# Full-height second score products and deinterleaved up weights in a hybrid decoder block with 32 experts

## Chip, core and metric

One core of one Trainium2 chip. The metric is the device time of one execution in microseconds; the median of several executions is given, and one further execution was profiled. Everything is computed in fp32 by splitting operands into a high and a low part (type fp32r) and adding three, or where one operand is packed two, products.

## The reference, cut to what matters

One layer on x of shape (1, 1024, 1024): a combined input projection feeds a stick-breaking attention (8 heads of 64) and an HGRN2 recurrence (4 heads of 128); both are projected, merged by sigmoid gates, projected again and normalised. Then a router picks 4 of 32 experts for each token, and each expert is a clamped SwiGLU. The two places that the change touches:

```python
def stick_breaking_attention(q, k, v):
    for blk in range(T // SB_BLOCK):                      # blocks of 128 queries
        t0, t1 = blk * SB_BLOCK, (blk + 1) * SB_BLOCK
        z = jnp.einsum('bhtd,bhsd->bhts', qf[:, :, t0:t1], kf[:, :, :t1]) * scale
        mask = jnp.arange(t1)[None, :] < (t0 + jnp.arange(SB_BLOCK))[:, None]
        log_keep = jnp.where(mask, jax.nn.log_sigmoid(-z), 0.0)
        log_after = lax.cumsum(log_keep, axis=3, reverse=True) - log_keep
        weights = jnp.where(mask, jnp.exp(jax.nn.log_sigmoid(z) + log_after), 0.0)
        outs.append(jnp.einsum('bhts,bhsd->bhtd', weights, vf[:, :, :t1]))

def expert_block(args):
    xblk, e = args
    hcat = xblk @ w_up[e] + b_up[e]                       # 1024 -> 2048
    x_glu = jnp.minimum(hcat[:, 0::2], SWIGLU_LIMIT)      # even columns
    x_lin = jnp.clip(hcat[:, 1::2], -SWIGLU_LIMIT, SWIGLU_LIMIT)
    act = x_glu * jax.nn.sigmoid(SWIGLU_ALPHA * x_glu) * (x_lin + 1.0)
    return act @ w_down[e] + b_down[e]
```

## The kernel before

The stages follow each other: projections of x and the HGRN chunks (to about 555 us of the span), the attention (to about 786 us), branch projections and merge, output projection and router (to about 1060 us), the experts (to about 2530 us), the last normalisation. `split` (L122) casts to the high part on ACT (L125) and subtracts it from the source on DVE or POOL (L126) to get the low part. `mm3` (L128) is the projections' triple of products (L130, L131, L132).

**Attention** (`sb_attention`, L551). Queries go in blocks of 128, i = 0 to 7; block i has 128 (i + 1) keys. A unit is a group of heads of one block (HEADS: 8, 4, 2, 2, 1, 1, 1, 1 heads), 43 units in all. The q tile of a block, 128 rows by 8 heads by 128 queries, holds a head's 64 channels twice: the high part on the rows of the head's own half (even heads 0 to 63, odd heads 64 to 127), the low part on the other half. `load_q` (L569) brings the raw queries, two transfers, `split_q` casts them (ACT, L576) and subtracts (DVE, L579). The keys' high part `kh` has them on both halves, the low part `kl` has the two heads of a pair on the two halves of one tile. So a score tile z takes two products: L611 on all 128 rows (high and low q with high k), and L612 on the 64 rows of the head's half (high q with low k). ACT turns z into `keep` and `take` by two sigmoids (L615, L616), POOL masks the diagonal (L620), DVE scans `keep` and multiplies it into `take` (L629, L631), PE transposes (L642), ACT or DVE copies (L645, L647), PE multiplies with v (L664, 64 columns wide).

```python
for s in range(n + 3):
    scores(s); stick(s - 1); turn(s - 2); average(s - 3)     # with yields between
```

`lockstep` (L70) mixes this stream with a second one, `beside` (L1688): the gate projections that are left (pj, L130 to L132) and then the turning of the branches (L730). It fixes the order of PE's instructions by estimated costs.

**Experts** (`experts`, `expert`). The experts are sorted by load; places 0 to 17 have capacities of 204 down to 134 tokens ("wide"), places 18 to 31 have 128. SEQ alternates wide and others. Weights come in raw pieces of 1 MB (six buffers, all on SP's queue, L1198); `part` splits a piece of 128 x 1024 into wh and wl (8 buffers each) six pieces ahead of its use, every fifth piece's subtraction on POOL, the others on DVE. In a wide expert the weight is the stationary operand. Its up product takes even columns (g = 0) and odd ones (g = 1) apart, each with 128 columns of the piece, every second word:

```python
for g in range(2):
    nc.tensor.matmul(ps[g][:, :2 * n], wh[:, kk, g::2], x[:, k]...)       # L1220
    nc.tensor.matmul(ps[g][:, :n], wl[:, kk, g::2], x[:, k, 0], ...)      # L1222
```

The down product (`down_parted`, L1269 and L1271) has the same shapes with 128 words in a row. There are 18 x 16 = 288 wide up pieces with 8 such pairs each, 2304 pairs. The 14 other experts use the weight as the moving operand (L1303 to L1305).

Of the kernel before, what the change touches and what calls it, by code (L numbers as in the profile page):

```python
# [9 lines left out]
F32 = mybir.dt.float32  # L10
F32R = mybir.dt.float32r
# [10 lines left out]
KT = D // 128  # L22
# [38 lines left out]
SBH = 8  # L61
# [53 lines left out]
class Block:  # L115
# [382 lines left out]
    def sb_tiles(self):  # L498
# [3 lines left out]
        self.kl = sp.tile([128, 4, T], F32R, name="kl")  # L502
        self.sv = sp.tile([128, NB, 512], F32, name="sv")

    def sb_jobs(self):

        nc = self.nc
        self.q_d = self.dram("q_scratch", (512, T))

        def ev_k(c):  # L510
            def go(ps, ct, half):
                p = 2 * c + ct
                t = slice(512 * half, 512 * half + 512)
                for i in range(2):
                    r, o = slice(64 * i, 64 * i + 64), slice(64 - 64 * i, 128 - 64 * i)
                    self.split(self.kh[r, 2 * p + i, t], self.kl[r, p, t], ps[r])
                    (nc.vector.tensor_copy if i else nc.scalar.copy)(self.kh[o, 2 * p + i, t], ps[r])
            return go

        def ev_q(c):  # L520
            def go(ps, ct, half):
                s = self.work.tile([128, 512], F32, name="pe", bufs=2)
                nc.scalar.copy(s, ps)
                r = 256 * c + 128 * ct
                nc.gpsimd.dma_start(self.q_d[r:r + 128, 512 * half:512 * half + 512], s)
            return go

        def ev_v(c):
            def go(ps, tb):
                nc.vector.tensor_copy(self.sv[:, tb, 256 * c:256 * c + 256], ps)  # L530
            return go

        jobs = []
        for c in range(2):
            jobs.append((OFF_SQ + 256 * c, (0, 1), ev_q(c)))
            jobs.append((OFF_SK + 256 * c, (0, 1), ev_k(c)))
        jobs += [(OFF_SV + 256 * c, None, ev_v(c)) for c in range(2)]
        return jobs
# [18 lines left out]
    def sb_attention(self):  # L557

        nc, wk = self.nc, self.work
# [3 lines left out]
        after = dict(zip(BLOCKS, BLOCKS[1:]))  # L563
        st = {}

        def load_q(i):
            raw = wk.tile([128, SBH, 128], F32, name="qraw", bufs=2)
            for r in (slice(0, 64), slice(64, 128)):
                nc.sync.dma_start(raw[r], self.q_d[:, 128 * i:128 * i + 128].rearrange("(h p) t -> p h t", p=64))  # L569
            st["raw", i] = raw  # L570

        def split_q(i):

            q = wk.tile([128, SBH, 128], F32R, name="q", bufs=2)
            raw = st.pop(("raw", i))
            nc.scalar.copy(q, raw)  # L576
            for k in range(2):
                s = (slice(64 - 64 * k, 128 - 64 * k), slice(k, None, 2))
                nc.vector.tensor_tensor(q[s], raw[s], q[s].bitcast(F32), op=OP.subtract)  # L579
            st["q", i] = q  # L580

        def heads(u):

            i, h0 = units[u]
            h = range(h0, h0 + HEADS[i])
            return [*h[::2], *h[1::2]]

        def scores(u):
            i, h0 = units[u]
            m, S = HEADS[i], 128 * (i + 1)  # L590
            if u == 0:
                load_q(i)
                split_q(i)
            if i in after and h0 == 0:
                load_q(after[i])
            if i in after and h0 + m >= 6 and h0 < 6:
                split_q(after[i])
            q = st["q", i]
            take = wk.tile([128, T], F32, name="take", bufs=4)
            keep = wk.tile([128, T], F32, name="keep", bufs=3)  # L600
            per = max(1, min(m // 2, 512 // S))
            hs = heads(u)
            for g in range(0, m, per):
                for s0 in range(0, S, 512):
                    n = min(512, S - s0)
                    ps = self.sps.tile([128, 512], F32, name="z", bufs=2)
                    for k in range(per):
                        h = hs[g + k]
                        r = slice(64 * (h % 2), 64 * (h % 2) + 64)
                        o, s = ps[:, S * k:S * k + n], slice(s0, s0 + n)  # L610
                        nc.tensor.matmul(o, q[:, h], self.kh[:, h, s], start=True, stop=False)  # L611
                        nc.tensor.matmul(o, q[r, h], self.kl[r, h // 2, s], start=False, stop=True)  # L612
                    w = n + S * (per - 1)
                    d = slice(S * g + s0, S * g + s0 + w)
                    nc.scalar.activation(keep[:, d], ps[:, :w], AF.Sigmoid, scale=-0.125)  # L615
                    nc.scalar.activation(take[:, d], ps[:, :w], AF.Sigmoid, scale=0.125)  # L616

            for t, fill in ((keep, 1.0), (take, 0.0)):
                t = t[:, :m * S].rearrange("p (h s) -> p h s", h=m)[:, :, S - 128:]
                nc.gpsimd.affine_select(t, t, pattern=[[0, m], [-1, 128]], compare_op=OP.is_gt, fill=fill,  # L620
                                        base=0, channel_multiplier=1)
            st[u] = [keep, take]
# [58 lines left out]
        n = len(units)  # L681
# [473 lines left out]
    def expert(self, n, e, rows, bias, choice):  # L1155
        nc, wk, a = self.nc, self.work, self.a
        blocks = [(s, min(128, n - s)) for s in range(0, n, 128)]
        nb = len(blocks)
        wide, parted = n > 128, n >= PARTED
        f = "A" if wide else "B"  # L1160
        X = {}
# [39 lines left out]
        def part(kind, c, q, width, kn):  # L1201

            per = 2048 // width // kn
            r = X["raw", kind, c, q // per][:, kn * (q % per):kn * (q % per) + kn]
            wh = wk.tile([128, kn, width], F32R, name="wh", bufs=8)
            wl = wk.tile([128, kn, width], F32R, name="wl", bufs=8)
            self.pieces += 1
            self.split(wh, wl, r, nc.gpsimd if self.pieces % POOLED == 0 else nc.vector)
            X[kind, c, q] = wh, wl

        def up_wide(c, q):
            wh, wl = X.pop(("up", c, q))
            x = X["x"]
            if q == 0:
                X["ps"] = [self.eps.tile([128, 512], F32, name="mm", bufs=6) for g in range(2)]
            ps = X["ps"]
            for kk in range(4):
                k = 4 * q + kk
                for g in range(2):
                    nc.tensor.matmul(ps[g][:, :2 * n], wh[:, kk, g::2], x[:, k].rearrange("p a n -> p (a n)"),  # L1220
                                     start=k == 0, stop=False)
                    nc.tensor.matmul(ps[g][:, :n], wl[:, kk, g::2], x[:, k, 0], start=False, stop=k == KT - 1)  # L1222
            if q == 0:
                return
            if c == 0:
                X["a"] = wk.tile([128, KT, 2, n], F32R if parted else F32, name="aTA", bufs=1)
            gl = wk.tile([128, 2, 256], F32, name="gl", bufs=3)[:, :, :n]
            for g in range(2):
                nc.scalar.activation(gl[:, g], ps[g][:, n:2 * n], AF.Identity, bias=bias(g, c))  # L1229
                nc.vector.tensor_add(gl[:, g], gl[:, g], ps[g][:, :n])  # L1230
            nc.vector.tensor_scalar(gl[:, 0], gl[:, 0], SWIGLU_LIMIT, None, op0=OP.min)
            nc.vector.tensor_scalar(gl[:, 1], gl[:, 1], SWIGLU_LIMIT + 1.0, 1.0 - SWIGLU_LIMIT,
                                    op0=OP.min, op1=OP.max)
            X["gl", c] = gl
# [125 lines left out]
        def piece(product, kind, c, q, width, kn, parted=True, after=()):  # L1360
            per = 2048 // width // kn
            return ((fetch, kind, c, q // per, width) if q % per == 0 else None,
                    (part, kind, c, q, width, kn) if parted else None, (product, c, q), list(after))

        if wide:
            up = [piece(up_wide, "up", c, q, 256, 4, True,
                        [(1, gate_wide, c)] + [(2, part_wide, c)] * parted if q else [])
                  for c in range(8) for q in range(2)]
# [4 lines left out]
        else:  # L1373
            up = [piece(up_narrow, "up", c, q, 512, 2, True, [(1, gate_narrow, c), (3, turn_act, c)] if q == 3 else [])
                  for c in range(4) for q in range(4)]
# [382 lines left out]
```

## Time and profile before

| | |
|---|---|
| median of 3 runs | 2603.86 us (2602.51 to 2604.72) |
| the profiled execution's own time | 2603.79 us |
| its span | 2602.2 us |
| busy: PE, PE weight loads, DVE, ACT, POOL | 2464.0, 2180.7, 1870.6, 1454.7, 869.2 us |
| mean granted TensorE clock | 0.974 |

PE is TensorE's matmuls and PEld its weight loads, which overlap them; DVE, ACT, POOL and SP are the vector, scalar, GpSimd and sync engines. Matmuls are pipelined and their ends are modelled, so the time that one costs is read from its start to the next one's start. A view by windows gives busy time of each engine in a stretch, the mean granted clock as a share of full speed, the share of the 16 DMA engines' time and GB/s.

### The profile page before, as it was taken

Reading aid. Unit: us, or ns where it says so; the run is one execution under the profiler, and the core shown is the slowest. Engines: PE = TensorE matmul, PEld = TensorE weight load, DVE = VectorE, ACT = ScalarE, POOL = GpSimd, SP = SyncE. Lnnn points to the kernel's source line nnn. Section 1 sums busy time; section 2 is a strip of 40 time slices with the busy share of each in tenths; the row PEclk is TensorE's granted clock in tenths of the full one; section 3 lists DMA queues with packets and bytes.
Section 4 is the critical chain, followed back from the end, with each engine's and each line's share of the span. In section 5 each row is a group of like instructions: output and inputs, shape, how many; then the busy total and the mean of one; then the engine's idle time right before and its main releaser. Section 6 shows DMA issues by size and latency. Waiting matters only on the chain. (4 is left out here: it accounts for less than half of the span.)

```text
span 2602.2 us, 41853 instructions
## 1 busy us (share of the span) xinstructions
PE 2464.0 (95%) x15476; PEld 2180.7 (84%) x15476; DVE 1870.6 (72%) x3107; ACT 1454.7 (56%) x2513; POOL 869.2 (33%) x744
## 2 busy tenths in 40 slices
PE   8999999999989987799999999999999999999992
PEld 8898888886767765789989999999998999889981
DVE  3217673347775477687888789888888888888885
ACT  3213332325564311576777677776677777777772
POOL 1011110003221324344434344444444444444443
PEclk9999999999999998899999999999999999999996
DMA  5321233233123523898998989999899998999973
GB/s 165 96 81 53 79 109 101 65 77 96 51 86 114 175 89 112 261 304 285 302 310 292 286 272 305 314 302 290 272 305 299 312 299 287 302 308 321 320 226 138
DMA packets 426788, 550.57 MB, mean 212 GB/s; under 512 B 21382, under 2 KB 312342, under 8 KB 426580
## 3 DMA queue, kind: packets, MB, share of 16 engines
q1 hardware_dynamic: 403684, 476.76, 56.3%
q0 software_dynamic: 22608, 70.05, 9.4%
q8 instruction: 123, 2.02, 0.3%
q10 hardware_dynamic: 288, 1.05, 0.2%
q14 instruction: 85, 0.70, 0.1%
HBM read 496.33 MB, written 51.47 MB: 211 GB/s over the span
## 5 line engine op out<-in xcount | busy, mean ns | idle before, releaser
L126 DVE TENSOR_TENSOR wl<-raw,wh 128x1024 fp32r<-128x1024 f32 x671 | 882.8, 1329 | 201.9 <-ACT wh L125 197.8
L125 ACT CAST wh<-raw 128x1024 fp32r<-128x1024 f32 x824 | 845.0, 1046 | 70.7 <-PE pj L269 20.6
L1220 PE MATMUL mm<-xTA,wh 128*128 128x292 f32 (+16 forms) x2304 | 616.8, 355 | 0.0
L126 POOL TENSOR_TENSOR wl<-raw,wh 128x1024 fp32r<-128x1024 f32 x153 | 379.6, 2481 | 508.8 <-ACT wh L125 467.2
L1222 PE MATMUL mm<-xTA,wl 128*128 128x146 f32 (+16 forms) x2304 | 544.6, 236 | 0.0
L1222 PEld LDWEIGHTS mm<-xTA,wl 128*128 128x128 f32 x2304 | 454.9, 197 | 0.5
L1220 PEld LDWEIGHTS mm<-xTA,wh 128*128 128x128 f32 x2304 | 450.4, 196 | 0.8
L1269 PE MATMUL mm<-aTA,wh 128*128 128x292 f32 (+16 forms) x1152 | 299.4, 346 | 3.2 <-POOL aTA L126 3.2
L1271 PE MATMUL mm<-aTA,wl 128*128 128x146 f32 (+16 forms) x1152 | 270.9, 235 | 0.0
L1271 PEld LDWEIGHTS mm<-aTA,wl 128*128 128x128 f32 x1152 | 220.1, 191 | 0.6
L1269 PEld LDWEIGHTS mm<-aTA,wh 128*128 128x128 f32 x1152 | 216.6, 188 | 4.4 <-POOL aTA L126 3.9
L130 PE MATMUL pj<-xh,wh 128*128 128x512 f32 x512 | 209.5, 409 | 0.0
L126 POOL TENSOR_TENSOR aTA<-gl,aTA 128x146 fp32r<-128x146 f32 (+16 forms) x144 | 112.5, 789 | 285.0 <-ACT aTA L125 276.5
L132 PE MATMUL pj<-xh,wl 128*128 128x512 f32 x512 | 201.3, 393 | 0.0
L131 PE MATMUL pj<-xl,wh 128*128 128x512 f32 x512 | 200.7, 392 | 0.0
L1303 PE MATMUL mm<-wh,xTB 128*128 128x512 f32 x448 | 187.8, 419 | 0.0
L1305 PE MATMUL mm<-wh,xTB 128*128 128x512 f32 x448 | 176.3, 393 | 0.0
L1304 PE MATMUL mm<-wl,xTB 128*128 128x512 f32 x448 | 175.0, 391 | 0.0
L1229 ACT ACTIVATE gl<-mm,bup 128x146 f32<-128x146 f32 (+16 forms) x288 | 96.9, 388 | 116.9 <-PE mm L1222 115.0
L1239 DVE TENSOR_TENSOR gl<-gl 128x146 f32<-128x146 f32 (+16 forms) x144 | 113.6, 789 | 10.9 <-ACT gl L1238 10.7
L132 PEld LDWEIGHTS pj<-xh,wl 128*128 128x128 f32 x512 | 96.7, 189 | 21.4
L130 PEld LDWEIGHTS pj<-xh,wh 128*128 128x128 f32 x512 | 96.8, 189 | 20.7 <-issue 2.5
(350 smaller groups left out, 4664.5 us busy)
## 6 DMA issues: line engine op xcount, KB each, us to landing
raw<-in_expert_w_up_dram SPq DMA_DIRECT2D x252, 1024.0 KB
raw<-in_expert_w_down_dram SPq DMA_DIRECT2D x128, 1024.0 KB
raw<-in_w_in_dram SPq DMA_DIRECT2D x56, 512.0 KB
gate_scratch<-pe POOLq DMA_DIRECT2D x32, 256.0 KB
gate<-gate_scratch SPq DMA_DIRECT2D x8, 1024.0 KB
qf<-in_x_dram SPq DMA_DIRECT2D x8, 512.0 KB
qraw<-q_scratch SPq DMA_DIRECT2D x16, 256.0 KB
xt<-in_x_dram SPq DMA_DIRECT2D x8, 512.0 KB
```

Source lines behind the costliest of these rows:

```text
L125: nc.scalar.copy(hi, src)
L126: (engine or nc.vector).tensor_tensor(lo, src, hi.bitcast(F32), op=OP.subtract)
L130: nc.tensor.matmul(ps, wh, xh, start=start, stop=False)
L131: nc.tensor.matmul(ps, wh, xl, start=False, stop=False)
L132: nc.tensor.matmul(ps, wl, xh, start=False, stop=stop)
L1220: nc.tensor.matmul(ps[g][:, :2 * n], wh[:, kk, g::2], x[:, k].rearrange("p a n -> p (a n)"), start=k == 0, stop=False)
L1222: nc.tensor.matmul(ps[g][:, :n], wl[:, kk, g::2], x[:, k, 0], start=False, stop=k == KT - 1)
L1269: nc.tensor.matmul(ps[i][:, :2 * n], wh[:, kk, s], act[:, k].rearrange("p a n -> p (a n)"), start=k == 0, stop=False)
L1271: nc.tensor.matmul(ps[i][:, :n], wl[:, kk, s], act[:, k, 0], start=False, stop=k == KT - 1)
L1303: nc.tensor.matmul(p, x[:, k, 0], wh[:, kk], start=k == 0, stop=False)
L1304: nc.tensor.matmul(p, x[:, k, 0], wl[:, kk], start=False, stop=False)
L1305: nc.tensor.matmul(p, x[:, k, 1], wh[:, kk], start=False, stop=False)
```

## The change

In the attention two tiles `qz` of 128 rows by 4 heads by 128 queries are added, zeroed once on POOL. `own_q(i, g)` copies the high part of four heads of block i into `qz[g]`, each head's 64 rows alone, with two ACT copies; the other 64 rows stay zero. The second score product then runs on all 128 rows: the zeros meet the other head's keys. The raw q tile has one buffer in place of two. In the experts `part` reads a wide expert's up piece even columns first, then odd, and so writes wh and wl deinterleaved; the product takes 128 words in a row.

```diff
+        self.qz = [sp.tile([128, SBH // 2, 128], F32R, name=f"qz{i}") for i in range(2)]
+        for z in self.qz:
+            for k in range(2):
+                self.nc.gpsimd.memset(z[64 - 64 * k:128 - 64 * k, k::2].bitcast(F32), 0.0)
...
-            raw = wk.tile([128, SBH, 128], F32, name="qraw", bufs=2)
+            raw = wk.tile([128, SBH, 128], F32, name="qraw", bufs=1)
...
+        def own_q(i, g):
+            for k in range(2):
+                r = slice(64 * k, 64 * k + 64)
+                nc.scalar.copy(self.qz[g][r, k::2], st["q", i][r, 4 * g + k:4 * g + 4:2].bitcast(F32))
...
             if u == 0:
                 load_q(i)
                 split_q(i)
+                own_q(i, 0)
+            if h0 == 0:
+                own_q(i, 1)
...
-                        r = slice(64 * (h % 2), 64 * (h % 2) + 64)
                         o, s = ps[:, S * k:S * k + n], slice(s0, s0 + n)
                         nc.tensor.matmul(o, q[:, h], self.kh[:, h, s], start=True, stop=False)
-                        nc.tensor.matmul(o, q[r, h], self.kl[r, h // 2, s], start=False, stop=True)
+                        nc.tensor.matmul(o, self.qz[h // 4][:, h % 4], self.kl[:, h // 2, s], start=False, stop=True)
...
+            if i in after and h0 + m >= 6 and h0 < 6:
+                own_q(after[i], 0)
...
+            if wide and kind == "up":
+
+                r = r.rearrange("p k (i g) -> p k g i", g=2)
             wh = wk.tile([128, kn, width], F32R, name="wh", bufs=8)
             wl = wk.tile([128, kn, width], F32R, name="wl", bufs=8)
             self.pieces += 1
+            X[kind, c, q] = wh, wl
+            if wide and kind == "up":
+                wh, wl = (w.rearrange("p k (g i) -> p k g i", g=2) for w in (wh, wl))
             self.split(wh, wl, r, nc.gpsimd if self.pieces % POOLED == 0 else nc.vector)
-            X[kind, c, q] = wh, wl
...
-                    nc.tensor.matmul(ps[g][:, :2 * n], wh[:, kk, g::2], x[:, k].rearrange("p a n -> p (a n)"),
+                    nc.tensor.matmul(ps[g][:, :2 * n], wh[:, kk, 128 * g:128 * g + 128], x[:, k].rearrange("p a n -> p (a n)"),
                                      start=k == 0, stop=False)
-                    nc.tensor.matmul(ps[g][:, :n], wl[:, kk, g::2], x[:, k, 0], start=False, stop=k == KT - 1)
+                    nc.tensor.matmul(ps[g][:, :n], wl[:, kk, 128 * g:128 * g + 128], x[:, k, 0], start=False, stop=k == KT - 1)
```

The order of the instructions on PE and DVE stays as it is; the rows there have the same count. On ACT the copies come in. This is ACT at the start of the attention, before (q is the split q tile, keep and take the sigmoids of a unit's score tiles; the numbers tell tiles apart):

```order
L576 CAST q_4786<-qraw_4783 128x1024
L576 CAST q_4793<-qraw_4790 128x1024
L615 ACT_TABLE_LOAD
L615 ACTIVATE keep_4798<-z_4799 128x512
L616 ACTIVATE take_4797<-z_4799 128x512
L615 ACTIVATE keep_4798<-z_4810 128x512
L616 ACTIVATE take_4797<-z_4810 128x512
```

And now:

```order
L581 CAST q_4792<-qraw_4789 128x1024
L590 CAST qz0_3827<-q_4792 64x2x128 x2
L590 CAST qz1_3828<-q_4792 64x2x128 x2
L581 CAST q_4803<-qraw_4800 128x1024
L627 ACT_TABLE_LOAD
L627 ACTIVATE keep_4808<-z_4809 128x512
L628 ACTIVATE take_4807<-z_4809 128x512
L627 ACTIVATE keep_4808<-z_4820 128x512
L628 ACTIVATE take_4807<-z_4820 128x512
L590 CAST qz0_3827<-q_4803 64x2x128 x2
L590 CAST qz1_3828<-q_4803 64x2x128 x2
```

The first block's copies stand between the casts of block 0 and block 1; block 1's copies follow the sigmoids of the first unit. The cast of block 1 stands ahead of the first sigmoid in both.

On SP's queue the raw q loads of the first three blocks, before (in brackets what a row waits for):

```order
L569 DMA qraw<-q_scratch 64x8x128 [waits DMASW4_49,DMASW2_49,DMASW6_49,DMASW0_49,PE_49]
L569 DMA qraw<-q_scratch 64x8x128 x3
L569 DMA qraw<-q_scratch 64x8x128 [waits DMAHW5_49,DMAHW6_49,DVE_49,Activation_49]
L569 DMA qraw<-q_scratch 64x8x128 [waits DMAHW2_49]
L225 DMA raw<-in_w_in_dram 128x8x128 [waits DMAHW3_49]
```

And now:

```order
L574 DMA qraw<-q_scratch 64x8x128 [waits DMASW4_49,DMASW2_49,DMASW6_49,DMASW0_49,PE_49]
L574 DMA qraw<-q_scratch 64x8x128
L574 DMA qraw<-q_scratch 64x8x128 [waits DMAHW5_49,DMAHW6_49,DVE_49,Activation_49]
L574 DMA qraw<-q_scratch 64x8x128
L574 DMA qraw<-q_scratch 64x8x128 [waits DMAHW0_49,DMAHW7_49,DVE_49,Activation_49]
L574 DMA qraw<-q_scratch 64x8x128 [waits DMAHW2_49]
L225 DMA raw<-in_w_in_dram 128x8x128 [waits DMAHW3_49]
```

The second block's pair of loads now waits for DVE and ACT to be done with the first block's raw tile; the third block's did so before too, for the first block's, and now for the second's.

## Rows read from the trace of the kernel before

**Rows 1.** The page, part 1: busy us of each engine over the span.
```profile
PE 2464.0 (95%) x15476; PEld 2180.7 (84%) x15476; DVE 1870.6 (72%) x3107; ACT 1454.7 (56%) x2513; POOL 869.2 (33%) x744
```

**Rows 2.** Windows: length, busy PE, PEld, DVE, ACT, POOL; clock, DMA share, GB/s.
```profile
560.00:742.00 182.00, 178.89 (x1045) 126.26 (x1043) 137.60 (x144) 97.87 (x207) 45.48 (x86) 0.97 0.29 77
742.00:786.00 44.00, 35.90 (x248) 25.71 (x248) 37.84 (x35) 30.86 (x62) 14.04 (x17) 0.88 0.33 102
1060.00:2530.00 1470.00, 1456.25 (x9639) 1352.63 (x9638) 1242.38 (x1806) 1073.60 (x1777) 652.88 (x411) 1.00 0.92 296
```

**Rows 3.** Timeline of PE, projections: start us, us, engine, line, operation.
```profile
738.33 0.39 PE L131 MATMUL pj<-xl,wh 128*128 128x512 f32 x1
738.56 0.39 PE L132 MATMUL pj<-xh,wl 128*128 128x512 f32 x1
```

**Rows 4.** Timeline of PE, scores of 384 and 512 columns.
```profile
741.41 0.44 PE L611 MATMUL z<-kh,q 128*128 128x384 f32 x1
741.78 0.44 PE L612 MATMUL z<-kl,q 64*128 64x384 f32 x1
...
753.59 0.48 PE L611 MATMUL z<-kh,q 128*128 128x512 f32 x1
754.00 0.49 PE L612 MATMUL z<-kl,q 64*128 64x512 f32 x1
754.43 0.50 PE L611 MATMUL z<-kh,q 128*128 128x512 f32 x1
```

**Rows 5.** Tile z, its second product: ns min/median/max, first and last start, forms.
```profile
L612 PE MATMUL z<-kl,q x96: 322/482/502, 561.7 to 785.4; 64*128 64x512 f32 x48, 64*128 64x128 f32 x16, 64*128 64x256 f32 x16, 64*128 64x384 f32 x16
```

**Rows 6.** Windows of 20 us in the attention.
```profile
580.00:600.00 20.00, 18.13 (x105) 12.79 (x105) 17.62 (x23) 10.84 (x22) 6.91 (x10) 0.91 0.46 120
600.00:620.00 20.00, 20.00 (x119) 13.26 (x116) 14.71 (x18) 12.78 (x26) 4.88 (x9) 1.00 0.36 92
...
760.00:780.00 20.00, 16.96 (x113) 11.94 (x111) 19.58 (x19) 14.77 (x30) 7.67 (x9) 0.83 0.24 79
```

**Rows 7.** Groups by form, ACT: busy us, mean ns.
```profile
L125 ACT CAST aTB<-tr 128x256 fp32r<-128x256 f32 x56 | 21.0, 375 | 26.9 <-PE tr L1327 26.9
```

**Rows 8.** Timelines of SP, ACT and DVE at the attention's start.
```profile
548.58 15.16 SPq L569 DMA_DIRECT2D qraw<-q_scratch  x6
...
553.72 1.05 ACT L576 CAST q<-qraw 128x1024 fp32r<-128x1024 f32 x1 [14.49 <-DMA qraw<-q_scratch]
...
563.57 0.60 ACT L615 ACTIVATE keep<-z 128x512 f32<-128x512 f32 x1 [4.97 <-PE z L612]
...
560.68 2.84 DVE L579 TENSOR_TENSOR q<-qraw,q 64x512 fp32r<-64x512 f32 x4
```

**Rows 9.** The page, part 5: weight loads of the wide experts.
```profile
L1220 PEld LDWEIGHTS mm<-xTA,wh 128*128 128x128 f32 x2304 | 450.4, 196 | 0.8
...
L1269 PEld LDWEIGHTS mm<-aTA,wh 128*128 128x128 f32 x1152 | 216.6, 188 | 4.4 <-POOL aTA L126 3.9
```

**Rows 10.** Timeline of PE, one expert: first and last of 26 and of 23 pairs.
```profile
1704.86 0.35 PE L1220 MATMUL mm<-xTA,wh 128*128 128x312 f32 x1
...
1711.42 0.36 PE L1220 MATMUL mm<-xTA,wh 128*128 128x312 f32 x1
...
1717.65 0.34 PE L1269 MATMUL mm<-aTA,wh 128*128 128x312 f32 x1
...
1723.27 0.35 PE L1269 MATMUL mm<-aTA,wh 128*128 128x312 f32 x1
```

**Rows 11.** Groups of the experts (1060 to 2530 us): the split of a piece.
```profile
L126 DVE TENSOR_TENSOR wl<-raw,wh 128x1024 fp32r<-128x1024 f32 x609 | 809.3, 1340 | 150.0 <-ACT wh L125 146.2 <-DVE yT L1279 0.6 <-issue 0.3
L125 ACT CAST wh<-raw 128x1024 fp32r<-128x1024 f32 x762 | 782.7, 1046 | 13.5 <-DMA raw<-in_expert_w_up_dram 11.1 <-PE mm L1342 2.4
```

**Rows 12.** Groups by form, DVE: L332 contiguous sources, L381 every second word.
```profile
L332 DVE TENSOR_TENSOR pe<-pe,ng 128x256 f32<-128x256 f32 x16 | 6.8, 424 | 29.1 <-ACT pe L331 29.1
...
L381 DVE TENSOR_TENSOR qx<-qf 128x256 f32<-128x256 f32 x8 | 3.3, 415 | 0.0
```

**Rows 13.** Waits of ACT in the experts: us in total, times, longest us.
```profile
ACT wh L125 <- DMA raw<-in_expert_w_up_dram: 11.1, 3, 7.7
```

## The prediction

> **What bounds the kernel now.** The page's first part comes first: PE is busy 95% of the span [rows 1]. That is a mean over stages, so the long windows come next [rows 2]. The diff touches two stages. In the experts (1060 to 2530 us) PE works 1456.25 of 1470.00 us, DVE 1242.38, ACT 1073.60: PE is the bound there, and idles for 14 us in all. In the attention up to its last query block (560 to 742 us) PE works 178.89 of 182.00 us and DVE 137.60. In the last block (742 to 786 us) it is another picture: PE 35.90 and DVE 37.84 of 44.00, at a granted clock of 0.88. There nobody is full, PE and DVE hand work to each other (scan, multiply, transpose), and DVE gets to 0.86 of the time. That 0.86 is used below.
>
> The third view is the timeline of PE, for what a product really costs: from its start to the next one's start, since the ends are modelled. In the projections, all on 128 rows, it is 738.33 to 738.56, 0.23 us for 512 columns [rows 3]. In the scores of 512 columns it is 0.41 us from L611 to L612 and 0.43 us from L612 to L611 [rows 4]. The same array, the same columns, no idle time in the rows, and 0.19 us more at each step into and out of the 64-row product. With 384 columns the step is 0.37 us, where three quarters of 0.23 is 0.17: again 0.20 us more. So the loss does not scale with columns; it is a price of the change between 128 and 64 rows.
>
> **Part 1: the second score product on 128 rows.** There are 96 such products [rows 5], each entered and left once. Loss of a pair: 0.84 us less 2 × 0.23 = 0.38 us; 96 × 0.38 = 36.5 us. The zeros cost nothing, since a 64-row product of 512 columns streams as many columns as a 128-row one. By the shapes, blocks 0 to 6 have 80 pairs (8, 8, 8, 8, 16, 16, 16), 30.4 us of PE time, block 7 has 16, 6.1 us.
>
> How much of it reaches the end? From 560 to 742 us PE must do 178.9 − 30.4 = 148.5 us, DVE still 137.6. PE's need alone allows −30; but the stage becomes like that of the last block, two engines near full that hand work over. The row for that state gives DVE 0.86: 137.6 / 0.86 = 160 us, −22. The ends are −13 (DVE at 0.81: no row shows less where DVE sets the pace, I allow for it) and −30 (DVE at 0.91, and 760 to 780 us shows it at 19.58 of 20.00 [rows 6]). I take −22, since the row of 0.86 comes from the same loop a few us later. In block 7 PE already waits for DVE, so of 6.1 us I take 1; the ends are 0 and 6.
>
> A price of the new balance is the clock. In slices in which PE waited, the granted clock (a mean between its levels of 1.2 and 2.4 GHz) was 0.91 with 18.13 busy us of 20, right after the stage's start, and 0.83 with 16.96 [rows 6]; from 600 to 620 us, where PE had no gap, it was 1.00 [rows 6]. With PE at 148.5 of 160 us there will be gaps. I take +2 us; the ends are 0 and 6.
>
> The copies into the zero-padded tiles: 8 blocks × 2 groups × 2 halves = 32 on ACT, of 256 columns. The nearest row is a cast of 128x256, 0.375 us [rows 7]; 12 us in all, and ACT goes from 97.87 to 110 of some 160 us, 69%. What covers them is that ACT has no share in the bound. If that cover fails they delay the transposed weights' copies behind them on ACT by 0.75 us a block, 6 us in all. Each copy waits for DVE's subtraction in the q tile; that stands in DVE's order before the scans of the unit before, and in ACT's order the copies of the next block come after the scores' sigmoids, so the data is there. I take 0 (0 to +6). The four memsets on POOL, early, are free: POOL is busy 45.48 of 182.00 us in the attention [rows 2].
>
> One raw q buffer in place of two. SP now issues six q transfers in a row at 548.58, the first cast is at 553.72, 5.1 us later, and DVE subtracts both blocks' from 560.68, 0.7 us each [rows 8]. With one buffer the second load goes out only when the first block's subtraction is done, at about 562.1; it lands some 5.1 us later, at 567.2. Its cast stands on ACT ahead of the table load and the first sigmoid, so that one moves from 563.57 to about 569.6, by 6 us. On SP two w_in loads stand behind it, for gate projections later than that. On PE the two score tiles of the first unit are written already and projections follow, so it goes on; but DVE's first scan starts 6 us late and it is DVE that I just made the limit. I take +3 (0 to +6). Later blocks load a whole block ahead: 0.
>
> Attention: −22 − 1 + 2 + 0 + 3 = −18 us.
>
> **Part 2: deinterleaved up weights.** 18 wide experts × 128 = 2304 pairs L1220/L1222 read every second word of the weight tile as stationary; L1269/L1271, the down products, have the same columns and read 128 words in a row. Their loads take 196 and 188 ns [rows 9]. Over whole pairs of one expert, 1704.86 to 1711.42 is 25 pairs of the up product, 262.4 ns each, and 1717.65 to 1723.27 is 22 pairs of the down product, 255.5 ns each [rows 10]. So 6.9 ns a pair, 2304 × 6.9 = 16 us. The bound below is the loads' difference alone, hidden beside the matmul: 0; above, 8 ns for each of 4608 loads: 37. I take the 16 of whole pairs, and since PE has next to no idle time there, but waits now and then for another engine, −15 of them arrive.
>
> What pays is the split. ACT's cast and the subtraction of 288 up pieces read the raw tile with every second word. ACT's cast is 1.046 us, DVE's subtraction 1.340 [rows 11]. A row with the same kind of read exists on DVE: L381 multiplies two sources of every second word, 128x256, in 415 ns; L332 with contiguous sources takes 424 [rows 12]. So the price on DVE is 0. For ACT and POOL no row shows it. Bounds: 0 by the row on DVE; above, one more column time for each skipped word, which for ACT is (1.046 − 0.375) / 768 = 0.87 ns, +0.89 us a piece, × 288 = 257 us: ACT at 1331 of 1470. Even that would leave ACT below PE. I take 0. Here a page speaks against the change: the Trainium skill, "Vector Engine (DVE) Microarchitecture Reference", section "Measured stream behaviour on trn2", says that a DVE port keeps its full rate only over runs of two adjacent words, and gives 1.73 ns a column instead of 1.054 when one source hops at each element; by that each piece would cost 0.69 us more, an estimate from that page. Row L381 disagrees, with runs of one word at 415 ns for 256 columns [rows 12].
>
> Transfers don't take the gain back: the DMA share is 0.92 at 296 GB/s [rows 2], 0.93 on a stage 15 us shorter, and ACT waited for a weight transfer three times, 11.1 us [rows 13].
>
> **The sum.** The profiled execution took 2603.79 us, the median of the runs is 2603.86, so the two are one number here. 2603.8 − 18 − 15 = 2571.
>
> **Rivals.**
> (a) Everything arrives: PE sheds 36.5 + 16 us and nothing else becomes late, 2551. For: PE is busy 178.89 of 182.00 us and 1456.25 of 1470.00 now [rows 2]. Against: DVE at 0.86 to 0.98 once PE waits.
> (b) The attention's gain is swallowed: the late first scan and the hand-over between DVE and PE leave −3 of −18. Then 2603.8 − 3 − 15 = 2586. For: DVE at 17.62 of 20 us from 580 to 600 [rows 6]. Against: 44 us of DVE idle time from 560 to 742.
> (c) The stationary's stride is not what makes the up pair longer (the loads lie beside the matmuls and the 6.9 ns come from elsewhere): only the attention counts, 2586.
> (d) The subtraction on DVE gets dearer by half, +0.67 us for each of 230 pieces (four of five of 288), 154 us: DVE 1396 of 1455, 96%, PE waits in the stretches where wide up pieces follow each other, the 15 us are lost and a few more: about 2592. The skill's rule above would do this.
> (e) Slower: strided reads run at half rate. On DVE a column costs (1.340 − 0.424) / 768 = 1.19 ns, +1.22 us a piece, × 230 = 281 [rows 11, 12]: DVE needs 1523 us, at 0.98 busy 1554, 84 more than now; 2603.8 − 18 + 84 = 2670. It decides from 0.80 us a piece on, (1455 × 0.98 − 1242) / 230. Against: row L381.
> (f) The 0.19 us is not the change of rows but something that stays (the reading of the q tile, say), and the experts give little: no change, 2602.
>
> **How the numbers follow.** Forecast 0.66; (a) 0.06, (b) 0.08, (c) 0.05, (d) 0.04, (e) 0.06, (f) 0.05. From 2554 to 2594 lie the forecast with its bounds (about 2560 to 2582), (b), (c) and (d), 0.83 in all; (a) lies just below and (e) and (f) above. A measurement of this kernel tells 0.2%, 5.2 us, from no change. Faster by more than that: the forecast and (a) to (d), 0.89; within it: (f), 0.05; slower: (e), 0.06.
>
> **What would show it.** Right: the step from the first to the second score product at 0.23 us for 512 columns; the attention's end some 18 us earlier, with DVE at 0.85 or more of it and PE below 0.95; pairs of the up product at 255 ns where the down product has them; cast and subtraction of up pieces as long as of down pieces. Wrong: the score step still at 0.4 us (f); the step short and the end of the attention where it was (b); up pieces longer than down pieces on DVE or ACT, and PE waiting for them (d, e).

## The result, and the profile after

The changed kernel takes 2575.48 us (median of 4 runs, 2572.58 to 2581.29), the kernel before, run beside it, 2603.19 us. The ratio is 0.9896 with a 95% interval from 0.9878 to 0.9915: 28 us faster. The profiled execution took 2572.58 us, its span is 2570.9 us, 31.3 us less than before; it is the fastest of the four.

Where the 31.3 us lie, by the first and last start of lines: the last score product starts at 769.5 us in place of 785.4 (−15.9), the output projection at 874.4 in place of 889.8 (−15.4), the first up product at 1042.5 in place of 1059.9 (−17.4), the last down product of a wide expert at 2514.1 in place of 2545.9 (−31.8). So the attention gave 16 us, the stage from the output projection to the experts 2, the experts 14.4. In the runs below the middle one of these three, which no edit touches, takes 167 to 173 us (170 before), so its 2 us cannot be told from its spread.

PE's timeline of the changed kernel around 718 us answers to [rows 3, 4]; L623 and L624 are the old L611 and L612 (columns: start us, us, engine, line, operation).

```profile
718.20 0.39 PE L623 MATMUL z<-kh,q 128*128 128x512 f32 x1
718.43 0.39 PE L624 MATMUL z<-kl,qz 128*128 128x512 f32 x1
718.66 0.34 PE L623 MATMUL z<-kh,q 128*128 128x384 f32 x1
718.83 0.34 PE L624 MATMUL z<-kl,qz 128*128 128x384 f32 x1
```

The step is 0.23 us for 512 columns and 0.17 for 384, just what a projection's product costs. The windows answer to [rows 2]: blocks 0 to 6, block 7, experts (length; busy PE, PEld, DVE, ACT, POOL; clock, DMA share, GB/s).

```profile
560.00:725.00 165.00, 153.47 (x1062) 125.43 (x1061) 138.92 (x144) 110.43 (x237) 55.32 (x86) 0.97 0.34 90
725.00:770.00 45.00, 32.72 (x239) 26.68 (x238) 36.77 (x35) 30.65 (x62) 14.22 (x17) 0.81 0.27 84
1042.00:2498.00 1456.00, 1438.55 (x9641) 1334.31 (x9640) 1241.68 (x1805) 1100.18 (x1778) 659.29 (x411) 1.00 0.93 299
```

From the first score product to block 7's first it was 561.4 to 743.77, 182.4 us; it is 562.14 to 725.41, 163.3 us. Block 7, from there to its last score product, went from 41.6 to 44.1 us, with the clock at 0.81 where it had 0.88. At the start of the attention PE now idles more. In its first two slices of 20 us PE was idle for 3.1 us before (the first of them here, the second in [rows 6]) and is for 10.6 us now. Before:

```profile
560.00:580.00 20.00, 18.76 (x63) 13.24 (x62) 11.09 (x20) 7.32 (x13) 4.20 (x6) 0.83 0.55 119
```

And now:

```profile
560.00:580.00 20.00, 13.23 (x62) 10.94 (x61) 9.16 (x15) 8.97 (x15) 3.48 (x4) 0.83 0.50 106
580.00:600.00 20.00, 16.19 (x102) 12.98 (x102) 18.35 (x24) 13.67 (x28) 6.70 (x9) 0.91 0.23 67
```

The timelines there answer to [rows 8], on ACT, DVE and PE:

```profile
554.52 1.05 ACT L581 CAST q<-qraw 128x1024 fp32r<-128x1024 f32 x1 [14.57 <-DMA qraw<-q_scratch]
555.60 1.68 ACT L590 CAST qz<-q 64x256 fp32r<-64x256 f32 x4
568.12 1.04 ACT L581 CAST q<-qraw 128x1024 fp32r<-128x1024 f32 x1 [10.84 <-DMA qraw<-q_scratch]
569.18 1.28 ACT L627 ACT_TABLE_LOAD   x1
570.47 0.60 ACT L627 ACTIVATE keep<-z 128x512 f32<-128x512 f32 x1
...
561.40 1.41 DVE L584 TENSOR_TENSOR q<-qraw,q 64x512 fp32r<-64x512 f32 x2
569.19 1.41 DVE L584 TENSOR_TENSOR q<-qraw,q 64x512 fp32r<-64x512 f32 x2 [6.39 <-ACT q L581]
...
571.61 0.39 PE L623 MATMUL z<-kh,q 128*128 128x256 f32 x1 [4.68 <-ACT take L628]
```

The second block's cast waits 10.84 us for its transfer, which waited for DVE's subtraction at 561.40; ACT's first sigmoid moves from 563.57 to 570.47; and PE stands for 4.68 us before the second unit's scores, since both score tiles are full.

In the experts, the pairs of one expert answer to [rows 10] and the groups of the whole span to [rows 9, 11]. L1239 is the up product, L1288 the down product (groups: busy us, mean ns, idle time before).

```profile
1680.07 0.34 PE L1239 MATMUL mm<-xTA,wh 128*128 128x312 f32 x1
...
1687.22 0.34 PE L1239 MATMUL mm<-xTA,wh 128*128 128x312 f32 x1
...
1693.43 0.34 PE L1288 MATMUL mm<-aTA,wh 128*128 128x312 f32 x1
...
1699.04 0.35 PE L1288 MATMUL mm<-aTA,wh 128*128 128x312 f32 x1
```

```profile
L126 DVE TENSOR_TENSOR wl<-raw,wh 128x1024 fp32r<-128x1024 f32 x671 | 882.1, 1328 | 203.9 <-ACT wh L125 201.6
L125 ACT CAST wh<-raw 128x1024 fp32r<-128x1024 f32 x824 | 871.5, 1079 | 69.6 <-PE pj L269 20.6 <-issue 20.0 <-DMA raw<-in_expert_w_up_dram 15.7
...
L126 POOL TENSOR_TENSOR wl<-raw,wh 128x1024 fp32r<-128x1024 f32 x153 | 379.9, 2483 | 508.6 <-ACT wh L125 471.2
...
L1239 PEld LDWEIGHTS mm<-xTA,wh 128*128 128x128 f32 x2304 | 433.6, 188 | 2.3 <-DVE gl L1249 1.4
```

28 pairs of the up product take 7.15 us, 255.4 ns each, and 22 of the down product 5.61 us, 255.0 ns. The up pair is now as short as the down pair. This is one expert; over all 17 widths of the moving operand the medians of the pairs make 18 us in 2304 pairs. The strided read costs DVE nothing (1.328 us, before 1.329 on the page) and POOL nothing (2.483, before 2.481); ACT's mean over all 824 casts rises from 1.046 to 1.079 us, which on the 288 up pieces is 0.09 us each.

### The profile page after: what moved, and what is told of

It reads as the page before. It is cut to its first block, busy times and chain, and to the rows that moved or that the text cites. A ratio compares the mean times of both kernels' runs of the same rounds, so it can differ in the third digit from the quotient of the medians.

```text
span 2570.9 us, 41878 instructions
## 1 busy us (share of the span) xinstructions
PE 2418.7 (94%) x15476; PEld 2164.0 (84%) x15476; DVE 1870.6 (73%) x3107; ACT 1493.0 (58%) x2545; POOL 887.3 (35%) x748
## 5 line engine op out<-in xcount | busy, mean ns | idle before, releaser
L125 ACT CAST wh<-raw 128x1024 fp32r<-128x1024 f32 x824 | 871.5, 1079 | 69.6 <-PE pj L269 20.6
L1239 PE MATMUL mm<-xTA,wh 128*128 128x292 f32 (+16 forms) x2304 | 598.1, 346 | 0.9 <-DVE gl L1249 0.9
L1241 PEld LDWEIGHTS mm<-xTA,wl 128*128 128x128 f32 x2304 | 440.5, 191 | 0.6
L1239 PEld LDWEIGHTS mm<-xTA,wh 128*128 128x128 f32 x2304 | 433.6, 188 | 2.3 <-DVE gl L1249 1.4
L1288 PE MATMUL mm<-aTA,wh 128*128 128x292 f32 (+16 forms) x1152 | 301.0, 347 | 3.9 <-POOL aTA L126 3.9
L1288 PEld LDWEIGHTS mm<-aTA,wh 128*128 128x128 f32 x1152 | 217.5, 189 | 5.1 <-POOL aTA L126 4.6
L126 POOL TENSOR_TENSOR aTA<-gl,aTA 128x146 fp32r<-128x146 f32 (+16 forms) x144 | 118.1, 828 | 264.9 <-ACT aTA L125 256.9
L1371 POOL DMA_INDIRECT acc_scratch<-yo,ti x50 | 98.9, 1979 | 40.2 <-ACT yo L1311 16.8
```

What stands on the lines that cost most here:

```text
L125: nc.scalar.copy(hi, src)
L126: (engine or nc.vector).tensor_tensor(lo, src, hi.bitcast(F32), op=OP.subtract)
L1239: nc.tensor.matmul(ps[g][:, :2 * n], wh[:, kk, 128 * g:128 * g + 128], x[:, k].rearrange("p a n -> p (a n)"), start=k == 0, stop=False)
L1241: nc.tensor.matmul(ps[g][:, :n], wl[:, kk, 128 * g:128 * g + 128], x[:, k, 0], start=False, stop=k == KT - 1)
L1288: nc.tensor.matmul(ps[i][:, :2 * n], wh[:, kk, s], act[:, k].rearrange("p a n -> p (a n)"), start=k == 0, stop=False)
```

## The experiments

**Each part alone.** The first run keeps the attention's part of the change and undoes the weights', the second the other way round. Both diffs are cut and shown against the changed kernel; `r` is the slice of the head's 64 rows.

```diff
-                r = r.rearrange("p k (i g) -> p k g i", g=2)
...
-                    nc.tensor.matmul(ps[g][:, :2 * n], wh[:, kk, 128 * g:128 * g + 128], ...
+                    nc.tensor.matmul(ps[g][:, :2 * n], wh[:, kk, g::2], ...
```

> The attention part alone; the experts read their weights as before. Theory (the parts are independent, the attention gives what its stage shows): 15 to 18 us below the kernel before, about 2586 us; first to second score product 0.23 us apart for 512 columns, PE still idle some 9 us between 560 and 600 us. Rival (the stage's gain is given back in the stages behind it, and the experts carry the whole change): 2598 to 2603 us.

Measured: 2584.71 us beside 2604.03, ratio 0.9926 (0.9913 to 0.9940), 19.3 us, a little more than expected. The attention ends as in the changed kernel (last score product at 767.4), PE idles 8.7 us between 560 and 600 us, and the experts take 1484.6 us from the first up product to the last down product, before 1486.0.

```diff
-                        nc.tensor.matmul(o, self.qz[h // 4][:, h % 4], self.kl[:, h // 2, s], start=False, stop=True)
+                        nc.tensor.matmul(o, q[r, h], self.kl[r, h // 2, s], start=False, stop=True)
```

> The deinterleaved up weights alone; the attention as before. Theory (6.9 ns for each of 2304 pairs, nearly all of it arrives): 14 to 16 us below the kernel before, about 2588 us; attention as before to 0.5 us. Rival (the dearer strided cast on ACT takes a part of it): less than 8 us below, and PE waits for wh or wl that it did not wait for.

Measured: 2595.29 us, ratio 0.9965 (0.9951 to 0.9978), 8.7 us. The two parts add up: 28 us together, as the whole change. But the weights give 9 where 14 to 16 were expected; their experts take 1476.7 us, where the changed kernel's profiled execution takes 1471.6. The windows of the second run show four slices of 20 us behind the stage's first in which the clock fell:

```profile
1738.00:1758.00 20.00, 17.78 (x96) 15.19 (x95) 19.03 (x28) 14.31 (x23) 8.30 (x6) 0.91 1.06 333
1858.00:1878.00 20.00, 16.59 (x106) 16.10 (x106) 16.23 (x23) 10.26 (x18) 5.43 (x3) 0.83 0.80 273
1978.00:1998.00 20.00, 17.76 (x96) 15.17 (x95) 18.68 (x26) 14.06 (x22) 7.20 (x4) 0.91 1.04 318
2220.00:2240.00 20.00, 19.21 (x102) 16.65 (x102) 14.62 (x18) 13.30 (x17) 8.54 (x6) 0.91 0.84 270
```

In the kernel before there were two (and in the changed kernel's profiled execution there are two again, each at 0.91):

```profile
1760.00:1780.00 20.00, 18.36 (x92) 15.87 (x93) 14.44 (x19) 13.25 (x18) 8.26 (x6) 0.91 0.90 287
2220.00:2240.00 20.00, 17.88 (x91) 15.03 (x90) 15.64 (x21) 13.56 (x21) 5.46 (x3) 0.91 1.01 324
```

PE's timeline of the second run in the slice at 0.83 (L1332 is the transpose of a narrow expert's activation, L1274 the down product):

```profile
1863.47 0.69 PE L1332 MATMUL tr<-idn,gl 128*128 128x128 f32 x2 [3.41 <-DVE gl L1324]
...
1864.34 0.54 PE L1274 MATMUL mm<-aTA,wh 128*128 128x304 f32 x1
...
1869.01 0.54 PE L1274 MATMUL mm<-aTA,wh 128*128 128x304 f32 x1
...
1870.75 0.34 PE L1274 MATMUL mm<-aTA,wh 128*128 128x304 f32 x1
...
1872.25 0.34 PE L1274 MATMUL mm<-aTA,wh 128*128 128x304 f32 x1
```

PE waited 3.41 us for DVE's activation. After it 10 pairs take 4.67 us, 467 ns each, and a little later 6 pairs take 1.50 us, 250 ns each: TensorE ran at 1.2 GHz, half of 2.4, for some 6 us, and lost 12 pairs' 0.22 us, 2.6 us. PE has four waits of over 2 us for this activation, at the same four places in both kernels. Before, they were 2.10, 2.46, 2.15 and 2.12 us, and a stretch at half clock came with the first and the last alone. In the second run they are 2.22, 3.41, 2.24 and 2.23 us, and one comes with each. A slice at 0.91 has lost 0.09 of its 20 us, 1.8 us, so the slices lost 3.6 us before and 8.8 us in the second run. So the count closes: 18 us less work, 3.8 us more waiting of PE in the stage (18.8 in place of 15.0), 5.2 us more lost at half clock, leaves 9.0; the stage gained 9.2. That the half clock comes from these waits is read from where the stretches lie; why it comes with one wait and not with another of the same length is not shown.

**The price of the strided cast.** The split reads in order again, the product still takes 128 words in a row.

```diff
-            if wide and kind == "up":
-                r = r.rearrange("p k (i g) -> p k g i", g=2)
```

> The changed kernel without the deinterleaving: the split reads and writes the up piece in order, the product still takes 128 words in a row, so even and odd columns are not told apart (this part of the computation is left out). Theory (ACT's strided cast is 0.09 us dearer than a plain one, off the bound): within 2 us of the changed kernel, the cast back at 1.046 us. Rival (the dearer cast costs PE time): 5 us or more below the changed kernel.

Measured: 2576.44 us, ratio 0.9889 (0.9873 to 0.9904), against 0.9896 for the change: no difference. The cast is back at its old price:

```profile
L125 ACT CAST wh<-raw 128x1024 fp32r<-128x1024 f32 x824 | 844.8, 1046 | 72.1 <-PE pj L269 20.6 <-issue 20.0 <-DMA raw<-in_expert_w_up_dram 15.7
```

So ACT's 26.5 us (871.5 less 845.0) are hidden, and they are not what the weights' part lacks. PE's four waits for the activation are there as well (2.2 to 3.2 us), so the strided read does not make them.

**The second raw q buffer.** In place of a second buffer beside the padded tiles, the first block's raw q goes into one of the four take tiles, which nobody needs yet.

```diff
-            raw = wk.tile([128, SBH, 128], F32, name="qraw", bufs=1)
+            raw = wk.tile([128, SBH, 128], F32, **(dict(name="qraw", bufs=1) if i else dict(name="take", bufs=4)))
```

> The changed kernel, with the raw q of the first block alone in a buffer of the take tiles, so that the second block's load need not wait for the first block's subtraction. Theory (the late second load holds up ACT's first sigmoid and then DVE's chain): first sigmoid back from 570.5 to about 564 us, and 5 us less in the end (3 to 9), about 2570 us. Rival (the late start is hidden by PE's projections, the DVE chain is long enough anyway): within 1.5 us of the changed kernel.

Measured: 2569.30 us, ratio 0.9869 (0.9850 to 0.9887), 6 us below the change. The first sigmoid is back at 563.21:

```profile
557.07 1.05 ACT L581 CAST q<-qraw 128x1024 fp32r<-128x1024 f32 x1
...
563.21 0.60 ACT L627 ACTIVATE keep<-z 128x512 f32<-128x512 f32 x1 [3.79 <-PE z L624]
```

```profile
560.00:718.00 158.00, 152.01 (x1066) 124.81 (x1066) 138.28 (x144) 108.77 (x237) 55.94 (x87) 0.98 0.34 92
718.00:762.00 44.00, 31.27 (x231) 25.42 (x230) 36.19 (x34) 29.85 (x59) 13.53 (x16) 0.81 0.27 82
```

Block 7's first score product comes at 717.80; blocks 0 to 6 take 155.7 us, 7.5 less than in the change, with DVE busy 0.88 of the stretch. Block 7 takes 44.0 us, as in the change.

**The row count alone.** No padded tile and no copy.

```diff
-                        nc.tensor.matmul(o, q[r, h], self.kl[r, h // 2, s], start=False, stop=True)
+                        nc.tensor.matmul(o, q[:, h], self.kl[:, h // 2, s], start=False, stop=True)
```

> The second product on all 128 rows straight from the q tile, without padded tiles, copies and with two raw q buffers as before (the scores then also hold the low q of a head times the low k of its neighbour, which is not left out as it should be); up weights deinterleaved. Theory (the 0.19 us steps vanish with the 64-row product, whatever feeds it, and the 32 copies are hidden): within 2 us of the run with the first block's raw q in a take tile, about 2569 us, score steps 0.23 us for 512 columns. Rival 1 (the copies on ACT hold up what stands behind them): 5 us or more below that run. Rival 2 (the steps come from reading q and not from the row count): score steps still 0.4 us and about 2590 us.

Measured: 2572.61 us beside 2603.46, ratio 0.9874 (0.9859 to 0.9889). The run with the first block's raw q in a take tile had 0.9869: this one is 3.3 us above it where at most 2 were expected, but their executions overlap (2569.36 to 2575.39 and 2565.66 to 2574.90), so no difference is shown. The step is short with the q tile itself:

```profile
717.54 0.39 PE L612 MATMUL z<-kl,q 128*128 128x512 f32 x1
717.77 0.34 PE L611 MATMUL z<-kh,q 128*128 128x384 f32 x1
```

So it is the row count that costs the 0.19 us, and the 32 copies cost nothing that can be measured: without them the kernel is not faster.

**Is DVE the limit in the attention?** All copies of transposed weights on ACT, on top of the first block's raw q in a take tile.

```diff
-                if u % 4 == 0:
+                if False:
                     nc.vector.tensor_copy(wt[:, :n], ps[:, :n])
```

> As the run with the first block's raw q in a take tile, and every copy of transposed weights on ACT, none on DVE, which takes some 14 us from DVE in the attention. Theory (DVE, at 0.88 from the first score to the last block, is what now limits the attention): 4 us or more below that run. Rival (PE still sets the pace in blocks 0 to 6): within 2 us of it, or above, since ACT has more to do.

Measured: 2561.16 us, ratio 0.9843 (0.9828 to 0.9858), 8 us below. The two profiled executions differ by 11.3 us. In them the attention, from first to last score product, goes from 199.7 to 194.6 us: 3.3 of it in blocks 0 to 6, where DVE is busy 6.9 us less (131.4 in place of 138.3), and 1.9 in block 7. So DVE's work is a part of the limit there, not all of it. The rest lies behind the attention, 4.1 of it in the experts (1476.6 to 1472.5 us), where nothing was changed; there, behind the stage's first, two stretches at half clock are left of four.

**The second stream's weight.** Less of the second stream ahead of block 7.

```diff
-LW2 = 0.57
+LW2 = 0.5
```

> As the run with the first block's raw q in a take tile, and the weight of the second stream 0.50 in place of 0.57, so that less of its work stands between the units of the early blocks and more is left for the last block. Theory (PE runs dry in the last block, at a clock of 0.74 to 0.83, since the second stream's products are used up there): 2 to 6 us below that run, more PE work and a higher clock in the last block. Rival (the early blocks are limited by DVE and have no room to go faster): the same within 1.5 us, or later.

Measured: 2573.17 us, ratio 0.9884 (0.9869 to 0.9899), 4 us slower than without it. The last score product comes at 760.7, a microsecond earlier, but the stream now ends behind it and the last v product moves from 773.0 to 778.4. The rival was right as to the time. Yet what the theory said of block 7 came true: it takes 41.0 us in place of 44.0, with more PE work and a clock of 0.88 in place of 0.81.

```profile
720.00:761.00 41.00, 33.13 (x263) 27.89 (x261) 30.43 (x25) 25.08 (x50) 11.27 (x17) 0.88 0.38 116
```

**The waits in the experts.** Three up pieces of a wide expert ahead of the down products of the one before.

```diff
-            return 2 if CAPS[SEQ[q]] > 128 else 4
+            return 3 if CAPS[SEQ[q]] > 128 else 4
```

> As the run with the first block's raw q in a take tile, and three pieces of a wide expert's up product in place of two ahead of the down products of the expert before it. Theory (four waits of PE of 2.2 to 3.4 us for DVE's activation, each followed by a stretch at half clock in some runs, take what is missing of the 16 us of the weights): these four waits vanish, no slice of the experts below a clock of 0.97 but the first, and 8 to 14 us below that run. Rival (another wait takes their place, since DVE is as late as before): within 3 us.

Measured: 2558.17 us, ratio 0.9820 (0.9806 to 0.9834), 11 us below the run without it; the experts take 1466.2 us in place of 1476.6. PE's waits (us in total, times, longest) in the run without, and in this one:

```profile
PE tr L1346 <- DVE gl L1338: 14.9, 12, 3.4
```

```profile
PE tr L1346 <- DVE gl L1338: 7.5, 8, 3.4
PE mm L1288 <- POOL aTA L126: 3.9, 4, 1.9
```

Three of the four waits are gone; the one of 3.4 us stays. One of PE's waits for POOL near the end of the stage grows from 1.3 to 1.9 us, and two slices still fall to a clock of 0.83, one at each of these two waits. So most of the gain is waiting (7.4 us) and little of it clock. The price was as expected, the picture only in part.

**Together.** The three edits in one kernel:

> The changed kernel with three edits together: the first block's raw q in a take tile, every copy of transposed weights on ACT, three up pieces ahead of the down products of the expert before. Theory (the waits lie in different stages, so their prices add: 6, 8 and 11 us): about 2550 us. Rival (the late activation in the experts or the start of the merge gives a part back): 2555 us or more.

Measured: 2551.43 us beside 2604.14, ratio 0.9797 (0.9784 to 0.9810). The prices add, to 25 us by the single runs and 24 here.

The same without padded tiles and copies, with the q tile itself as above:

> The same three edits' places without padded tiles and copies: the second product takes the q tile itself (the low q of a head times the low k of its neighbour is added, as in the run that did so before), two raw q buffers, every copy of transposed weights on ACT, three up pieces ahead. Theory (the copies into the padded tiles are hidden): within 2 us of the run with the three edits. Rival (now that ACT carries all copies it is near its limit, and 32 copies of 0.4 us cost): 4 us or more below it.

Measured: 2554.14 us, ratio 0.9803 (0.9790 to 0.9816): 2.7 us above, a little over the 2 expected, with executions that overlap. It is not faster, so the copies are hidden here too.

With POOLED = 4 in place of 5:

> The three edits, and every fourth piece's subtraction on POOL in place of every fifth: some 40 pieces move, 50 us off DVE and 100 us onto POOL over the whole kernel. Theory (the waits of PE that are left in the experts are for DVE's activation): 2 to 5 us below the run with the three edits. Rival (POOL's subtraction at 2.48 us a piece comes late, PE waits for it): slower than that run.

Measured: 2547.34 us (2546.60 to 2549.15), ratio 0.9782 (0.9769 to 0.9796), 4 us below, and the fastest kernel of this study. The reason given does not hold: PE's waits for the activation are 9.4 us in place of 7.5, and the experts take 1464.3 us in place of 1463.5. DVE has 39 pieces less but not less work, since each takes longer (the run with the three edits first):

```profile
L126 DVE TENSOR_TENSOR wl<-raw,wh 128x1024 fp32r<-128x1024 f32 x671 | 886.4, 1336 | 197.6 <-ACT wh L125 195.2 <-issue 0.2
```

```profile
L126 DVE TENSOR_TENSOR wl<-raw,wh 128x1024 fp32r<-128x1024 f32 x632 | 899.2, 1435 | 187.5 <-ACT wh L125 184.0 <-issue 0.2
```

A subtraction during which POOL works on nothing takes 1.22 us in both runs. One that overlaps with an instruction on POOL by more than 0.3 us takes 1.50 us on average with the three edits (282 of them) and 1.69 us here (293). In the profiles the gain lies ahead of the experts: the first up product starts at 1026.6 us in place of 1030.3. The edit changes nothing but the experts' pieces, and how it gives 4 us there stays open.

With LW2 = 0.62 in place of 0.57:

> The three edits, and the second stream's weight 0.62 in place of 0.57. Theory (0.50 was 4 us slower because the stream then ended behind the attention; a larger weight gets the branch turning done earlier): 1 to 3 us below the run with the three edits. Rival (the last block runs drier still, at a lower clock): 2 us or more above.

Measured: 2562.45 us, ratio 0.9837 (0.9824 to 0.9851), 11 us slower than the three edits: the last score product moves from 758.1 to 767.8, and PE is busy 12.75 of 20 us there at a clock of 0.67.

```profile
740.00:760.00 20.00, 12.75 (x83) 10.13 (x83) 11.73 (x9) 8.74 (x17) 5.55 (x6) 0.67 0.08 26
```

## Why the prediction was right, point by point

The time, 2575.5 us against 2571 forecast and a range from 2554 to 2594, came out by the mechanisms named, with terms that were off in both directions. That the sum is nearer than its terms is luck: blocks 0 to 6 gave 4.6 us more than forecast, and the raw buffer took 4.5 us more. Rivals (a), 2551, and (b), with an attention that gives 3 us, are out.

- **The score step.** Right: 0.41 us fell to 0.23 us, and the run with the q tile itself shows that the row count alone does it. The loss is the same 0.19 us at 256, 384 and 512 columns; at 128 columns, a sixth of the products, it is 0.14 (0.255 us fell to 0.113), so 35 us of PE time in place of 36.5. Rival (f) is out.
- **Blocks 0 to 6: −22.** Too small. With the first block's raw q in a take tile, which takes the other term away, they go from 182.35 to 155.74 us and gain 26.6. DVE is busy 0.88 there, not 0.86 (and 0.84 in the changed kernel, whose start is late). That DVE's work now sets a part of the pace is shown by the run that took its copies away: 6.9 us less of it gave 3.3. The lower end was also miscounted: 137.6 / 0.81 is 170 us, −12, not −13.
- **One raw buffer: +3, at most 6.** This step failed in size. The shift of the first sigmoid was right (569.6 forecast, 570.47 measured), but "so it goes on", said of PE, was wrong: both score tiles were full and PE stood for 4.68 us. The price is 7.5 us in the profiles, outside the ends that were given, and 6 in the medians, at the upper end.
- **Block 7: −1, and the clock: +2.** Together +1; measured +2.5. The block does not gain from 6.1 us less PE work, it loses: its clock falls from 0.88 to 0.81 as PE has more gaps. That the clock makes the loss is argued, and the run with the second stream's weight at 0.50 bears it out: with more PE work left for the block its clock is 0.88 again, and it takes 41.0 us. The clock's price came in this block and not in blocks 0 to 6, which kept 0.97.
- **The copies: 0.** Right in the end: 0.40 us each on ACT in place of 0.375, and the runs without them are not faster. One reason given was wrong: they do not wait for DVE's subtraction. They read the half of the q tile that the subtraction does not write, and start at 555.60, right behind the cast and 5.8 us ahead of the subtraction. PE waited for a copy once, 0.85 us, at the late second unit.
- **Attention: −18.** Measured −15.9 at the last score product in the profiled execution, −17.9 there in the one with this part alone, and −19.3 for the whole kernel with this part alone.
- **The weights' pair: 6.9 ns, 16 us of PE.** Right: 262.4 fell to 255.4 ns, and all widths together make 18 us. Rival (c) is out.
- **−15 of them arrive.** This term was too large. 14.4 us arrived in the profiled execution, 9.2 and 8.7 in the profile and the median of the run with this part alone. The words "waits now and then for another engine" stood for PE's four waits of 2.1 to 2.5 us for DVE's activation; they grew to 2.2 to 3.4 us as PE's work shrank, and in the run with this part alone all of them were followed by a stretch at half clock, where two had been. The run with three pieces ahead gains 11 us at these waits, but 8.8 us of them were there in the kernel before, and three pieces ahead were not tried on that kernel: not all of the 11 us are what the weights lacked.
- **The strided split: 0 on all engines.** DVE and POOL: right. ACT pays 0.09 us a piece, between the ends given; the run that reads in order shows that it is hidden. Rivals (d) and (e) are out. By the rule of the Trainium skill ("Vector Engine (DVE) Microarchitecture Reference", "Measured stream behaviour on trn2") DVE's mean over all pieces would have risen by some 0.2 us, an estimate from that page. It went from 1.329 to 1.328, so the rule does not hold here for a stride of two words.

The four executions of the changed kernel spread over 8.7 us. Those of the kernel before spread over 3.1 us in the four beside them, but over 7.7, 8.6 and 6.4 us in the three sets of nine beside the experiments, so a wider spread after the change is not shown. The experts of the changed kernel and of two runs with the same instructions there take 1471.6, 1476.6 and 1472.5 us, with two, four and two stretches at half clock behind the stage's first: these stretches are one part of the spread.

## What to carry to other kernels

A product on fewer rows than its neighbours costs a step at each change, here 0.19 us both ways for 256 to 512 columns and 0.14 for 128; if the missing rows can be filled with zeros (or with something too small to matter) at no cost in columns, fill them. When an engine that was the bound gets faster, price what it will wait for from the place where it already waits, and add the clock that the waits cost. A buffer that is given up to make room for the new tile is part of the change and can take back a quarter of its gain: look for a tile that is idle at that moment.

## What the runs showed of the hardware

- From a product on 128 rows to one on 64 rows, and back, a step of 512 columns takes 0.41 to 0.43 us; between products on 128 rows it takes 0.23 us, with the same tiles read.
- ACT reads every second word of an SBUF tile 9% slower (0.09 us on a cast of 1.046), DVE and POOL as fast as words in a row.
- TensorE's weight load of every second word takes 196 ns where words in a row take 188, and the pair of products is longer by 7.0 ns.
- A wait of PE of 2 to 3.4 us is followed by a stretch at 1.2 GHz in some cases (467 ns a pair in place of 250, for about 6 us after a wait of 3.41 us; also after waits of 2.10 and 2.12 us) and not in others (none after 2.46 and 2.15 us).
- With 192 pieces on POOL in place of 153, DVE's subtraction of the same shape rose from 1.336 to 1.435 us on average. It takes 1.22 us while POOL works on nothing, and the rise lies in those that overlap with POOL.
